# A chunked delta-rule recurrence on one core: two runs of small matrix products per chunk where there were three

## The chip, the cores and the metric

The kernel runs on one core of a Trainium2 chip. Its engines work side by side, each with an instruction queue of its own: PE multiplies matrices (PEld is its weight load), DVE, ACT and POOL do elementwise work, SP issues DMA transfers (ACT and POOL issue some too). An engine takes its instructions in the order in which the program gives them; it stands still when the next one waits for a semaphore. The metric is device time in microseconds.

## The reference, cut to what matters

The program is one layer of a decoder over 1024 positions of width 1024: a projection, three branches (the RWKV-7 recurrence, stick-breaking attention, cross-attention into 256 memory tokens), sigmoid gates with an output projection, and a convolutional feed-forward part. The change lies in the recurrence, for 8 heads of 64:

```python
def step(S, inp):
    r_t, w_t, k_t, v_t, kk_t, a_t = inp
    sa = jnp.einsum('bhij,bhj->bhi', S, -kk_t)
    S = (S * w_t[:, :, None, :]
         + sa[..., None] * (kk_t * a_t)[:, :, None, :]
         + v_t[..., None] * k_t[:, :, None, :])
    y_t = jnp.einsum('bhij,bhj->bhi', S, r_t)
    return S, y_t
...
y = rwkv7_recurrence(rh, dh, kh, vh, kk, ah)
```

Everything is float32, and the output is the layer's (1, 1024, 1024).

## The kernel before, in words

**Chunks.** The recurrence is computed in 16 chunks of 64 positions. What needs no state is prepared for all chunks in earlier stages: matrices of decayed products between positions (tiles `L`, read from DRAM into tags `at` and `it`), the values (`V`) and a triangular inverse (`TT`, in tag `qk`). The 8 heads stand as 4 pairs, one head on partitions 0 to 63 and one on 64 to 127. `stage2` (L599) then walks the chunks. For a chunk it does, on PE unless another engine is named, with one PSUM bank per pair (tag `g`, four banks) that is divided into four blocks of 64 columns, A, Y, W and S:

1. *A*: the state's part `ra` x U (8 products, one per head, from chunk 1 on) and on top the part M x v (8). DVE copies A of each pair into `v1` (L656).
2. *W*: the inverse applied to `v1` (8 products). ACT copies each head's W into the value tile, where it stands below the values (L664, 8 copies).
3. *Y* and *S*: the state's part of Y (8), then for each pair Y (2) and S (2), with both halves of the value tile, so of 128 rows. DVE updates the pair's state in place, U = U x decay + S (L674), and ACT copies Y of both heads into the output tile `y` (L676).

Chunk 0 has no state parts, and chunk 15 no S. A step reads what the step before it gave to another engine, and the next chunk's A reads the updated state.

**Large products between.** The steps are a generator; after each step it yields. `weave` takes one step, and then a number of steps of a second generator, `pump`, which does independent work: projections, gates and output products of the branches, six products of 128 x 128 by 128 x 512 at a time (`mm3`, L107). The ratio, 2.08 steps of six per yield, says how many. Every such instruction goes through `pinned` (L124), which with `strict` on fixes the order of each engine as the one in which the Python code emits it; so the code's order in `stage2` is the order on PE, ACT and DVE. All matrix products are recorded at one line, `mmul` (L139): the small ones write tag `g`, the large ones of this stage tag `mm`. `norm_part` yields pieces of the output's group norm (DVE and ACT), of which `next(norm, None)` takes one.

**Waits.** Tiles are tracked by the framework: an instruction that touches a buffer that another engine has read or written gets a semaphore wait for it.

**Around it.** Before `stage2`, `inverse` (L581) runs on DVE in 62 steps on the tile `inst`, which is loaded from `mad` by four DMAs (L578, one per pair, at the end of the preparation), and whose result goes to DRAM as `td` by sixteen DMAs (L597). They are issued by POOL. SP issues nearly all other loads: the weight tiles `wr` (L79) that feed the large products (split by ACT into `wh`, L83, and by POOL into `wl`, L89), the branch outputs `A` (L1261), the tiles `L` (L617).

Of the kernel before, what the change touches and what calls it, by code (L numbers as in the profile page):

```python
# [22 lines left out]
NC = T // C  # L23
# [27 lines left out]
class Trunk:  # L51
# [365 lines left out]
    def rwkv_prep(self, p, krv, need):  # L417
# [160 lines left out]
        nc.gpsimd.dma_start(self.inst[p * 32 : p * 32 + 32], self.mad[p * 32 : p * 32 + 32])  # L578
        yield

    def inverse(self):  # L581
# [11 lines left out]
        for p in range(4):  # L593
            for h2 in range(2):
                for cc in range(2):
                    i0 = p * 32 + h2 * 16 + cc
                    nc.gpsimd.dma_start(self.td[p // 2, :, h2, :, p % 2, cc * 64 : cc * 64 + 64], X[i0 : i0 + 15 : 2])  # L597
                    for _ in range(3):
                        yield  # L599

    def stage2(self):
        nc = self.nc
        self.y = [self.t4("qk") for _ in range(4)]
        uv = self.t4("ys", n=512).rearrange("p (u c) -> p u c", u=8)
        U, v1s = [uv[:, p] for p in range(4)], [uv[:, 4 + p] for p in range(4)]
# [29 lines left out]
        for c in range(NC):  # L635
            g, cc = c // 2, c % 2
            us = []
            for p in range(4):
                L, (V, TT) = Ls[g, p], VTs[g, p]
                us.append((  # L640
                    U[p], L[:, cc * 128 : (cc + 1) * 128], L[:, 256 + cc * 128 : 256 + (cc + 1) * 128],
                    L[:, 512 + cc * 256 : 512 + (cc + 1) * 256], [v[:, cc * 64 : (cc + 1) * 64] for v in V],
                    TT[:, cc * 64 : (cc + 1) * 64], v1s[p], self.ps("g")))

            def state(o, rs):
                for p, h2 in heads if c else ():
                    Up, ra, _, _, _, _, _, pb = us[p]
                    q = hq[h2]
                    self.mmul(pb[q, o], ra[q, rs], Up[q], start=True, stop=False)

            state(A, Y)
            for p, h2 in heads:
                _, _, _, M, wv, _, v1, pb = us[p]
                self.mmul(pb[hq[h2], A], M[hq[h2], h2 * 128 + 64 : h2 * 128 + 128], wv[h2][hq[h2]], start=(c == 0), stop=True)
                if h2 == 1:
                    self.pinned(nc.vector.tensor_copy(v1, pb[:, A]))  # L656
            yield
            next(norm, None)
            for p, h2 in heads:
                _, _, _, _, wv, tt, v1, pb = us[p]  # L660
# [6 lines left out]
            state(Y, A)  # L667
            for p, (Up, ra, bt, M, wv, tt, v1, pb) in enumerate(us):
                for h2, q in enumerate(hq):
                    self.mmul(pb[q, Y], M[:, h2 * 128 : h2 * 128 + 64], wv[h2], start=(c == 0), stop=True)  # L670
                if c < NC - 1:
                    for h2, q in enumerate(hq):
                        self.mmul(pb[q, S], bt[:, q], wv[h2], start=True, stop=True)
                    self.pinned(nc.vector.scalar_tensor_tensor(Up, Up, self.pc[p][:, c : c + 1], pb[:, S], ALU.mult, ALU.add))  # L674
                for h2, q in enumerate(hq):
                    self.pinned(nc.scalar.activation(self.y[p][cc * 64 : cc * 64 + 64, g * 128 + h2 * 64 : g * 128 + h2 * 64 + 64], pb[q, Y], AF.Copy))  # L676
            if cc and g + 2 < NG:
                for p in range(4):
                    load(g + 2, p)
            yield  # L680
            next(norm, None)
# [5 lines left out]
            if c == 13:  # L687
                self.gs = [self.load_gg(p) for p in range(2)]
        for _ in range(3):
# [1277 lines left out]
    def run(self):  # L1967
# [5 lines left out]
        self.bufs_w = {"w4": 3, "A": 4, "qk": 8, "at": 7, "ys": 1, "it": 1}  # L1973
# [72 lines left out]
        self.weave(st2, pump, 2.08, 0)  # L2046
# [83 lines left out]
```

## Time and profile before

| | us |
|---|---|
| time, median of 3 runs | 1788.42 (1787.28 to 1788.75) |
| the profiled execution: span | 1785.0 |
| PE busy in it | 1775.7 |
| window of the recurrence, 784.7 to 980.0 | 195.3 |
| PE busy in that window | 194.56 |

The span of a profiled execution is from its first to its last instruction on the core. It lies 3.4 us below the runs' median, and a time worked out on the span is compared with the runs by adding that.

How to read the rows that follow in the prediction. A *window* row gives start and end, length, and then for PE, PEld, DVE, ACT and POOL the busy time (with the count of instructions), then PE's granted clock, the DMA engines' busy share and GB/s. A row of the *timeline* or of the *chain of waits* gives a start, a duration, the engine (ACTq or SPq is that engine's queue of DMA issues), the line, the operation, output<-input, how many instructions it lumps, and in brackets the idle time before them with what ended it. One small float32 product leaves two records, so `x16` is 8 small products; some records can be missing. Rows of groups give the busy time and the mean of one instruction in ns, then the idle time ahead. `issue` is time in which an engine waited for nothing that the profile shows. A row "PE g L139 <- DVE ys L656" in the view of waits gives the idle time of the first engine that the second ended: the sum, the count and the longest.

### The profile page before, as it was taken

To read this page: it belongs to the slowest core of one execution; us is meant where nothing else is said; L and a number is where in the kernel's file an instruction comes from. 1 tells how busy PE (TensorE), PEld (TensorE's weight loads), DVE (VectorE), ACT (ScalarE), POOL (GpSimd) and SP (SyncE) were. 2 spreads that over 40 slices of the span, in tenths; PEclk is the share of its full clock that TensorE was granted. 3 is DMA by queue.
4 is the path that set the end of the run, shared out by engine and by line. 5 is a ranking of instruction groups with operands and counts; after the bars stand their busy time and mean duration, and the time that the engine had idled before them with its cause. 6 is when DMAs were issued, how large, how long until landed. Compare 5 with 4: busy or idle time off the path is not lost.

```text
span 1785.0 us, 27451 instructions
## 1 busy us (share of the span) xinstructions
PE 1775.7 (99%) x10481; PEld 1442.9 (81%) x10481; DVE 1184.1 (66%) x1687; ACT 882.8 (49%) x1667; POOL 697.1 (39%) x409
## 2 busy tenths in 40 slices
PE   9999999999999999999999999999999999999999
PEld 7777778878888888787777888888888888888887
DVE  5666674787888655243533882697767777795596
ACT  6543344466566635444556434454444445444343
POOL 1232252322221012022333322257777677545454
PEclk9999999999999999999999999999999999999999
DMA  4256574111112343658764662323323333396475
GB/s 185 72 167 188 180 247 152 51 56 43 54 57 69 111 126 93 201 181 280 264 229 146 236 210 98 115 89 124 101 89 110 109 109 113 109 330 219 142 248 200
DMA packets 120758, 263.39 MB, mean 148 GB/s; under 512 B 28330, under 2 KB 41130, under 8 KB 120499
## 3 DMA queue, kind: packets, MB, share of 16 engines
q1 hardware_dynamic: 82434, 193.31, 32.9%
q10 hardware_dynamic: 34416, 55.72, 8.5%
q0 software_dynamic: 3776, 12.62, 2.4%
q8 instruction: 82, 1.34, 0.3%
q14 instruction: 50, 0.40, 0.1%
HBM read 180.04 MB, written 81.53 MB: 147 GB/s over the span
## 4 chain that ended last, share of the span: by engine, by line
PE 62%; issue 1%; POOL 1%; ACT 1%; DVE 1%; DMA 0%; ACTq 0%; DVEq 0%; POOLq 0%; SPq 0%
PE mm L139 53%; PE g L139 8%; PE g L122 1%; POOL dw L1856 1%; DVE qk L715 0%; ACT wh L83 0%; DMA qk<-vd 0%; ACT w L885 0%; DVE w L886 0%; DVE keep L1876 0%; POOL l L1555 0%; ACT qk L664 0%; ACT ys L1020 0%; DVE wl L86 0%; ACT qk L1059 0%
## 5 line engine op out<-in xcount | busy, mean ns | idle before, releaser
L89 POOL TENSOR_TENSOR wl<-wr,wh 128x1024 fp32r<-128x1024 f32 x58 | 148.0, 2552 | 368.2 <-ACT wh L83 360.5
L139 PE MATMUL mm<-xhi,wh 128*128 128x512 f32 x784 | 260.6, 413 | 0.5 <-ACT w L936 0.4
L139 PE MATMUL mm<-xlo,wh 128*128 128x512 f32 x784 | 243.5, 392 | 0.7 <-DVE xlo L225 0.6
L139 PE MATMUL mm<-xhi,wl 128*128 128x512 f32 x784 | 242.2, 390 | 0.0
L139 PEld LDWEIGHTS mm<-xlo,wh 128*128 128x128 f32 x784 | 147.0, 188 | 34.0 <-DVE xlo L225 1.6
L139 PEld LDWEIGHTS mm<-xhi,wl 128*128 128x128 f32 x784 | 147.1, 188 | 32.6
L139 PEld LDWEIGHTS mm<-xhi,wh 128*128 128x128 f32 x784 | 136.5, 189 | 30.4 <-issue 7.9
L139 PE MATMUL mm<-dw,da 128*128 128x512 f32 x528 | 121.1, 390 | 0.0
L83 ACT ACTIVATE wh<-wr 128x1024 fp32r<-128x1024 f32 x75 | 79.5, 1060 | 81.0 <-PE mm L139 61.9
L139 PE MATMUL mm<-BT,l 128*128 128x512 f32 x504 | 118.0, 389 | 0.3 <-POOL l L1555 0.3
L139 PEld LDWEIGHTS mm<-dw,da 128*128 128x128 f32 x528 | 98.9, 188 | 21.7 <-DVE da L1855 1.2
L1856 POOL TENSOR_TENSOR dw<-draw,dw 128x512 fp32r<-128x512 f32 x55 | 83.1, 1520 | 77.0 <-ACT dw L1854 74.2
L985 DVE TENSOR_TENSOR_SCAN at<-at,at 128x128 f32<-128x128 f32 (+3 forms) x64 | 91.0, 1429 | 33.1 <-ACT at L979 33.0
L139 PEld LDWEIGHTS mm<-BT,l 128*128 128x128 f32 x504 | 94.5, 188 | 20.3 <-POOL l L1555 0.7
L139 PE MATMUL mm<-BT,wh 128*128 128x512 f32 x352 | 108.5, 389 | 0.1
L139 PE MATMUL mm<-B,wh 128*128 128x512 f32 x352 | 108.4, 389 | 0.0
L195 POOL TENSOR_TENSOR hf<-rs,half 128x16 f32<-128x16 f32 (+1 forms) x18 | 49.2, 2732 | 143.4 <-DVE rs L192 138.9
L1855 DVE TENSOR_TENSOR da<-draw,da 128x512 fp32r<-128x512 f32 x77 | 66.6, 873 | 49.0 <-ACT da L1853 48.6
L139 PE MATMUL g<-dw,da 128*128 128x512 f32 x396 | 90.5, 389 | 0.4 <-POOL dw L1856 0.4
L1853 ACT ACTIVATE da<-draw 128x512 fp32r<-128x512 f32 x77 | 48.3, 628 | 81.0 <-PE mm L139 31.7
L139 PEld LDWEIGHTS g<-dw,da 128*128 128x128 f32 x396 | 74.2, 188 | 16.2 <-POOL dw L1856 0.8
L1627 ACT ACTIVATE g<-u,params 128x512 f32<-128x512 f32 x88 | 65.2, 770 | 32.1 <-DVE u L1717 22.9
(345 smaller groups left out, 3956.6 us busy)
## 6 DMA issues: line engine op xcount, KB each, us to landing
wr<-in_w_in_dram SPq DMA_DIRECT2D x49, 512.0 KB, 3.8
draw<-actd SPq DMA_DIRECT2D x77, 256.0 KB, 3.1
at<-scr SPq DMA_DIRECT2D x28, 512.0 KB, 5.5
draw<-in_w_down_dram SPq DMA_DIRECT2D x55, 256.0 KB, 4.6
rw<-in_w_up_dram SPq DMA_DIRECT2D x22, 512.0 KB, 3.5
actd<-gall ACTq DMA_DIRECT2D x41, 256.0 KB, 3.1
gsd<-w ACTq DMA_DIRECT2D x20, 512.0 KB, 2.8
wr<-in_w_up_dram SPq DMA_DIRECT2D x18, 512.0 KB, 3.6
```

Source lines behind the costliest of these rows:

```text
L83: ins = self.nc.scalar.activation(hi, raw, AF.Copy)
L89: self.last_wl = self.nc.gpsimd.tensor_tensor(lo, raw, hi.bitcast(F32), ALU.subtract)
L122: self.pinned(self.nc.tensor.transpose(out, in_, self.ident[:n, :n]))
L139: self.pinned(self.nc.tensor.matmul(*a, **k))
L195: nc.gpsimd.tensor_tensor(out, t[:, :n], self.half[:, :n], ALU.pow)
L985: self.pinned(nc.vector.tensor_tensor_scan(sn[:, :W][:, ::-1], sn[:, :W][:, ::-1], self.smask[:, 1024 - W :][:, ::-1], 1.0, ALU.mult, ALU. ...
L1627: keep(nc.scalar.activation(c, u[:, 2 + h * 512 : 514 + h * 512], AF.Identity, scale=self.par("cw2", m), bias=self.par("cb", m)))
L1853: self.pinned(nc.scalar.activation(A[:, 0], a, AF.Copy))
L1855: self.pinned(nc.vector.tensor_tensor(A[:, 1], a, A[:, 0].bitcast(F32), ALU.subtract))
L1856: nc.gpsimd.tensor_tensor(Wt[:, 1], w, Wt[:, 0].bitcast(F32), ALU.subtract)
```

## The change

`stage2` does a chunk's steps in another order and in two runs in place of three. The step A for the next chunk (`head`) is no longer a run of its own: it follows directly on S, Y and the state's part of Y. Within the joined run S of all pairs comes first, then Y of all pairs, then the state's part of Y, pair by pair with ACT's copies, then the next chunk's A, its value part first and the state's part on top. The state has two copies, `uv` and `un`, which take turns (tag `ys` gets two buffers): the update reads one and writes the other, since the state's part of Y is now computed after the update. The four banks are taken once (`banks`), and chunks take turns in their two halves of 256 columns. There are two yields per chunk and one ahead, with 2.95 steps of large products each. The twenty transfers of `inverse` and of its input are issued by SP, and the descriptor area of the DMAs that POOL issues gets another size.

```diff
@@ end of the preparation (L578) and inverse (L597) @@
-        nc.gpsimd.dma_start(self.inst[p * 32 : p * 32 + 32], self.mad[p * 32 : p * 32 + 32])
+        nc.sync.dma_start(self.inst[p * 32 : p * 32 + 32], self.mad[p * 32 : p * 32 + 32])
...
-                    nc.gpsimd.dma_start(self.td[p // 2, :, h2, :, p % 2, cc * 64 : cc * 64 + 64], X[i0 : i0 + 15 : 2])
+                    nc.sync.dma_start(self.td[p // 2, :, h2, :, p % 2, cc * 64 : cc * 64 + 64], X[i0 : i0 + 15 : 2])
@@ stage2 @@
-        uv = self.t4("ys", n=512).rearrange("p (u c) -> p u c", u=8)
-        U, v1s = [uv[:, p] for p in range(4)], [uv[:, 4 + p] for p in range(4)]
+        uv, un = (self.t4("ys", n=512).rearrange("p (u c) -> p u c", u=8) for _ in range(2))
+        U, v1s = [[x[:, p] for p in range(4)] for x in (uv, un)], [uv[:, 4 + p] for p in range(4)]
...
-        for c in range(NC):
+        banks = [self.ps("g") for _ in range(4)]
+
+        def chunk(c):
...
-                    U[p], L[:, cc * 128 : (cc + 1) * 128], L[:, 256 + cc * 128 : 256 + (cc + 1) * 128],
+                    U[c % 2][p], U[1 - c % 2][p], L[:, cc * 128 : (cc + 1) * 128], L[:, 256 + cc * 128 : 256 + (cc + 1) * 128],
...
-                    TT[:, cc * 64 : (cc + 1) * 64], v1s[p], self.ps("g")))
-
-            def state(o, rs):
-                for p, h2 in heads if c else ():
-                    Up, ra, _, _, _, _, _, pb = us[p]
-                    q = hq[h2]
-                    self.mmul(pb[q, o], ra[q, rs], Up[q], start=True, stop=False)
-
-            state(A, Y)
+                    TT[:, cc * 64 : (cc + 1) * 64], v1s[p], banks[p][:, cc * 256 : cc * 256 + 256]))
+            return us
+
+        def head(c, us):
             for p, h2 in heads:
-                _, _, _, M, wv, _, v1, pb = us[p]
-                self.mmul(pb[hq[h2], A], M[hq[h2], h2 * 128 + 64 : h2 * 128 + 128], wv[h2][hq[h2]], start=(c == 0), stop=True)
+                _, _, _, _, M, wv, _, _, pb = us[p]
+                self.mmul(pb[hq[h2], A], M[hq[h2], h2 * 128 + 64 : h2 * 128 + 128], wv[h2][hq[h2]], start=True, stop=(c == 0))
+            for p, h2 in heads:
+                Up, _, ra, _, _, _, _, v1, pb = us[p]
+                if c:
+                    self.mmul(pb[hq[h2], A], ra[hq[h2], Y], Up[hq[h2]], start=False, stop=True)
                 if h2 == 1:
                     self.pinned(nc.vector.tensor_copy(v1, pb[:, A]))
-            yield
-            next(norm, None)
+
+        us = chunk(0)
+        head(0, us)
+        yield
+        for c in range(NC):
+            g, cc = c // 2, c % 2
             for p, h2 in heads:
...
             yield
             next(norm, None)
-            state(Y, A)
-            for p, (Up, ra, bt, M, wv, tt, v1, pb) in enumerate(us):
-                for h2, q in enumerate(hq):
-                    self.mmul(pb[q, Y], M[:, h2 * 128 : h2 * 128 + 64], wv[h2], start=(c == 0), stop=True)
-                if c < NC - 1:
+            if c < NC - 1:
+                for p, (Up, Un, _, bt, _, wv, _, _, pb) in enumerate(us):
                     for h2, q in enumerate(hq):
                         self.mmul(pb[q, S], bt[:, q], wv[h2], start=True, stop=True)
-                    self.pinned(nc.vector.scalar_tensor_tensor(Up, Up, self.pc[p][:, c : c + 1], pb[:, S], ALU.mult, ALU.add))
+                    self.pinned(nc.vector.scalar_tensor_tensor(Un, Up, self.pc[p][:, c : c + 1], pb[:, S], ALU.mult, ALU.add))
+            for p, (_, _, _, _, M, wv, _, _, pb) in enumerate(us):
                 for h2, q in enumerate(hq):
+                    self.mmul(pb[q, Y], M[:, h2 * 128 : h2 * 128 + 64], wv[h2], start=True, stop=(c == 0))
+            for p, (Up, _, ra, _, _, _, _, _, pb) in enumerate(us):
+                for h2, q in enumerate(hq):
+                    if c:
+                        self.mmul(pb[q, Y], ra[q, A], Up[q], start=False, stop=True)
                     self.pinned(nc.scalar.activation(self.y[p][cc * 64 : cc * 64 + 64, g * 128 + h2 * 64 : g * 128 + h2 * 64 + 64], pb[q, Y], AF.Copy))
+            if c < NC - 1:
+                us = chunk(c + 1)
+                head(c + 1, us)
...
-            yield
-            next(norm, None)
+            for _ in range(2):
+                next(norm, None)
...
+            yield
@@ run, main @@
-        self.bufs_w = {"w4": 3, "A": 4, "qk": 8, "at": 7, "ys": 1, "it": 1}
+        self.bufs_w = {"w4": 3, "A": 4, "qk": 8, "at": 7, "ys": 2, "it": 1}
...
-        self.weave(st2, pump, 2.08, 0)
+        self.weave(st2, pump, 2.95, 0)
...
-    nc = bacc.Bacc("TRN2", target_bir_lowering=False, num_devices=1)
+    nc = bacc.Bacc("TRN2", target_bir_lowering=False, num_devices=1, dynamic_dma_scratch_size=4096)
```

**The order on PE, before.** This is the end of one chunk's third run. `g_7263` to `g_7266` are the banks of the four pairs, `ys` is the state, `at` and `it` are the pair's tile `L`, `qk` its value tile; `Activation_49` and `DVE_49` are the semaphores of ACT and DVE.

```order
L139 MATMUL g_7265<-ys_6790,at_6986 64x64 [waits Activation_49]
L139 MATMUL g_7265<-ys_6790,at_6986 64x64
L139 MATMUL g_7266<-ys_6790,it_6992 64x64 [waits Activation_49]
L139 MATMUL g_7266<-ys_6790,it_6992 64x64
L139 MATMUL g_7263<-qk_6980,at_6978 64x64 x4
L139 MATMUL g_7264<-qk_6980,at_6984 64x64 x4
L139 MATMUL g_7265<-qk_6988,at_6986 64x64 x4
L139 MATMUL g_7266<-qk_6988,it_6992 64x64 x4
L139 MATMUL mm_7381<-yhi_6773,wh_7179 128x512 [waits DVE_49]
```

The state's part of Y stands first; its wait is for ACT's copies of the run before (W), ahead of which twelve large products stand. The sixteen products of Y and S (four per pair) have no wait in front of them, and large products follow.

**The same place on PE after the change.** The run begins with S of the four pairs; the rows are its next part, from the last pair's Y (read off `qk`) to the end of the state's part of Y.

```order
L139 MATMUL g_7029<-qk_6989,it_6993 64x64 [waits DVE_49]
L139 MATMUL g_7029<-qk_6989,it_6993 64x64
L139 MATMUL g_7026<-ys_6790,at_6979 64x64
L139 MATMUL g_7026<-ys_6790,at_6979 64x64 [waits Activation_49]
L139 MATMUL g_7027<-ys_6790,at_6985 64x64
L139 MATMUL g_7027<-ys_6790,at_6985 64x64 [waits Activation_49]
L139 MATMUL g_7028<-ys_6790,at_6987 64x64
L139 MATMUL g_7028<-ys_6790,at_6987 64x64 [waits Activation_49]
L139 MATMUL g_7029<-ys_6790,it_6993 64x64
L139 MATMUL g_7029<-ys_6790,it_6993 64x64 [waits Activation_49]
```

Each pair's Y has a wait for DVE in front of it, which resolves to that pair's state update from the same bank. The second head's state product of each pair waits for ACT, which resolves to the copy of the first head's Y. Right behind these rows, in the same run, stands the next chunk's A, value part:

```order
L139 MATMUL g_7026<-qk_6981,at_6979 64x64 x2
L139 MATMUL g_7027<-qk_6981,at_6985 64x64 x2
L139 MATMUL g_7028<-qk_6989,at_6987 64x64 x2
L139 MATMUL g_7029<-qk_6989,it_6993 64x64 [waits Activation_49]
L139 MATMUL g_7029<-qk_6989,it_6993 64x64
```

Its last pair waits for ACT, which resolves to the copy of that pair's last Y. Eight state products of A follow, and only then large products. The order holds 48 runs of small products before and 33 after, with 744 small products in both, and 18 large ones between most runs where there were mostly 12.

**The order on SP ahead of the recurrence.** Before:

```order
L621 DMA qk_6988<-vd 64x256
L622 DMA qk_6952<-td 128x256
L622 DMA qk_6980<-td 128x256
L1261 DMA A_6730<-yd 128x1024
L1261 DMA A_6732<-yd 128x1024
L79 DMA wr_6826<-in_w_in_dram 128x1024
L617 DMA at_6792<-scr 128x1024
L617 DMA at_6794<-scr 128x1024
L617 DMA at_6796<-scr 128x1024
L617 DMA at_6798<-scr 128x1024
L79 DMA wr_6888<-in_w_br_dram 128x1024
L1261 DMA A_6734<-yd 128x1024
```

And after:

```order
L79 DMA wr_6609<-in_w_in_dram 128x1024
L597 DMA td<-inst 8x64x64 x3
L1273 DMA A_6728<-yd 128x1024
L1273 DMA A_6730<-yd 128x1024
L1273 DMA A_6732<-yd 128x1024
L1273 DMA A_6734<-yd 128x1024
L79 DMA wr_6736<-in_w_in_dram 128x1024
L617 DMA at_6793<-scr 128x1024
```

The sixteen stores `td` have come into this queue, and the weight load `wr_6736`, which before was the row right ahead of those shown and had one of the four loads `A` ahead of it, now stands behind all four.

More of the change, by code (lines that the diff above doesn't have):

```diff
@@ L640, in stage2 @@
                 us.append((
-                    U[p], L[:, cc * 128 : (cc + 1) * 128], L[:, 256 + cc * 128 : 256 + (cc + 1) * 128],
+                    U[c % 2][p], U[1 - c % 2][p], L[:, cc * 128 : (cc + 1) * 128], L[:, 256 + cc * 128 : 256 + (cc + 1) * 128],
                     L[:, 512 + cc * 256 : 512 + (cc + 1) * 256], [v[:, cc * 64 : (cc + 1) * 64] for v in V],
-                    TT[:, cc * 64 : (cc + 1) * 64], v1s[p], self.ps("g")))
-            def state(o, rs):
-                for p, h2 in heads if c else ():
-                    Up, ra, _, _, _, _, _, pb = us[p]
-                    q = hq[h2]
-                    self.mmul(pb[q, o], ra[q, rs], Up[q], start=True, stop=False)
-            state(A, Y)
-            for p, h2 in heads:
-                _, _, _, M, wv, _, v1, pb = us[p]
-                self.mmul(pb[hq[h2], A], M[hq[h2], h2 * 128 + 64 : h2 * 128 + 128], wv[h2][hq[h2]], start=(c == 0), stop=True)
+                    TT[:, cc * 64 : (cc + 1) * 64], v1s[p], banks[p][:, cc * 256 : cc * 256 + 256]))
+            return us
+        def head(c, us):
+            for p, h2 in heads:
+                _, _, _, _, M, wv, _, _, pb = us[p]
[4 more added lines that the diff above has]
+                    self.mmul(pb[hq[h2], A], ra[hq[h2], Y], Up[hq[h2]], start=False, stop=True)
                 if h2 == 1:
                     self.pinned(nc.vector.tensor_copy(v1, pb[:, A]))
-            yield
-            next(norm, None)
+        us = chunk(0)
[3 more added lines that the diff above has]
+            g, cc = c // 2, c % 2
             for p, h2 in heads:
-                _, _, _, _, wv, tt, v1, pb = us[p]
+                _, _, _, _, _, wv, tt, v1, pb = us[p]
                 self.mmul(pb[hq[1 - h2], W], tt[hq[h2]], v1[hq[h2]], start=True, stop=True)
```

## The prediction, made before the changed kernel was run

> **What bounds the kernel now.** I read the page's first part, then the window of the stage that the change touches, then the chain of waits inside it, then who waited for whom on PE.
>
> ```profile
> span 1785.0 us, 27451 instructions
> PE 1775.7 (99%) x10481; PEld 1442.9 (81%) x10481; DVE 1184.1 (66%) x1687; ACT 882.8 (49%) x1667; POOL 697.1 (39%) x409
> 784.70:980.00 195.30, 194.56 (x2051) 152.69 (x2052) 77.24 (x235) 104.16 (x389) 61.78 (x37) 1.00 0.67 230
> 870.31 1.08 PE g L139 x32
> 871.39 2.95 PE mm L139 x12
> 874.34 0.61 PE g L139 x16
> 874.95 4.31 PE mm L139 x18
> 879.26 1.69 PE g L139 x48
> PE g L139 <- DVE ys L656: 0.5, 1, 0.5
> ```
>
> PE is busy 99% of the span, and 194.56 of the 195.30 us of the recurrence (third line: window, then PE, PEld, DVE, ACT and POOL busy). So the time is what PE has to issue plus every wait put in front of it. The next five lines are one chunk: three runs of small products (x16 records are 8 products, two records each) with 12 or 18 large ones between them. Those large products are the cover for the hand-offs between PE, DVE and ACT, and it suffices: in the whole recurrence PE itself waits once for another engine, 0.5 us. Whatever the change does is therefore decided by two questions: what a run costs beyond its products, and whether the hand-offs still lie under large products.
>
> **Part 1, fewer runs: a gain.** 8 products take 0.61 and 16 take 1.08, so 8 more cost 0.47 and a run of small products costs 0.14 more than its products. 18 large products take 4.31 and 12 take 2.95: 0.227 each, so a run of 12 (2.72) costs 0.23 more. A run removed is worth 0.14 + 0.23 = 0.37 us. The issue orders hold 48 runs of small products before and 33 after, with the same 744 products: 15 x 0.37 = **-5.5 us**. The cover ahead of the second and the third step grows from 12 to 18 large products, so what stalls there are go: the window leaves PE 195.30 - 194.56 = 0.74 us idle, **-0.7**.
>
> **Part 2, the hand-offs that now stand inside a run: a loss.** The rows of the issue order quoted with the change show it. In the joined run PE issues S for the four pairs, then Y, then the state part of Y, then the next chunk's A. Four Y products now wait for DVE (its update reads S from the same bank), the second half of each pair's state part waits for ACT (its copy of the first half), and the last pair's A waits for ACT's last copy. Before, PE wrote a pair's Y, state part and S in one go and DVE and ACT read the bank afterwards. What one hand-off takes:
>
> ```profile
> 788.36 0.68 PE L139 MATMUL g<-ys,qk 64*64 64x64 f32 x16
> 788.73 1.88 ACT L664 ACTIVATE qk<-g 64x64 f32<-64x64 f32 x8 [2.47 <-PE g L139]
> 791.91 1.15 PE L139 MATMUL g<-qk,at 128*64 128x64 f32 x32
> 792.49 0.97 DVE L674 SCALAR_TENSOR_TENSOR ys<-ys,pc,g 128x64 f32<-128x64 f32 x4 [5.48 <-PE g L139]
> L676 ACT ACTIVATE qk<-g x128: 216/219/222, 792.8 to 982.9; 64x64 f32<-64x64 f32 x128
> L674 DVE SCALAR_TENSOR_TENSOR ys<-ys,pc,g x60: 269/280/282, 792.5 to 969.7; 128x64 f32<-128x64 f32 x60
> 865.64 0.23 ACT qk L664
> 865.87 0.04 issue
> 865.91 1.41 PE g L139 x36
> 963.48 0.72 PE L139 MATMUL g<-ys,qk 64*64 64x64 f32 x16 [0.46 <-DVE ys L656]
> 964.13 0.73 PE L139 MATMUL mm<-xhi,wh 128*128 128x512 f32 x2
> ```
>
> A small product of 64 rows takes 0.47 / 8 = 0.059; of 128 rows (1.69 - 0.61) / 16 = 0.068. PE to ACT: ACT's copy waits for the second product, which goes off 0.06 after 788.36, and starts at 788.73: 0.31 from that product's start. PE to DVE: the update needs the fourth product after 791.91 (792.11) and starts at 792.49: 0.38. A copy is 0.22 and the next follows at 1.88 / 8 = 0.235; an update is 0.28, the next follows at (0.97 - 0.28) / 3 = 0.23. Back to PE: ACT ends at 865.87, PE starts at 865.91: 0.05.
>
> Y, counted from the first S: the pair's two S products end their issue so that DVE starts at 0.07 + 0.38 = 0.45; the four updates end at 0.73, 0.96, 1.19 and 1.42; the last pair's Y starts at 1.47 and is issued by 1.61. Without waits the 16 products are through at 16 x 0.068 = 1.08. **0.53 per chunk.**
>
> State part and next A: the first pair's second half may start 0.31 + 0.22 + 0.05 = 0.58 after the first. It and the next pair's first half then go off together, ACT makes two copies in a row, and the next second half starts 0.31 + 0.235 + 0.22 + 0.05 = 0.815 later; three times, 2.45. The last copy comes back after another 0.58, and only then may the last pair's A start: 0.58 + 2.45 + 0.58 = 3.61 from the first state product. Without waits 14 products stand there, 14 x 0.059 = 0.83. **2.78 per chunk.**
>
> Chunks 1 to 14 have both: 14 x 3.31 = 46.3. Chunk 0 has no state part, but its Y waits (0.53) and A must wait for eight copies that begin with the first Y (0.78 + 0.07 + 0.31 = 1.16; 1.16 + 1.88 + 0.05 = 3.09 against 1.08 + 6 x 0.059 = 1.43): 1.66. The last chunk has neither S nor A: 0.58 + 2.45 + 0.06 - 0.47 = 2.62. Together **+50.6**. These waits have no cover at all: the large products are queued behind them on PE, and PE passes nothing forward (at 963.48 it stood 0.46 us for DVE with large products next in its order).
>
> After a wait the products restart a little late: at 963.48 a run of 8 gave way to large products after 0.65 against 0.61 without a wait, 0.04. With nine waits in a joined run, 14 x 9 x 0.04 = **+5**.
>
> Copies and updates can also find their engine busy. In the window ACT works 104.16 us, of which 54.3 are these copies (28.0 and 26.3 by the groups below), so other work holds it 50 us, about a fifth of a stage that becomes 245 us long; its usual piece is 1.05.
>
> ```profile
> L664 ACT ACTIVATE qk<-g 64x64 f32<-64x64 f32 x128 | 28.0, 219 | 28.8 <-PE g L139 26.4 <-ACT w L889 0.4
> L676 ACT ACTIVATE qk<-g 64x64 f32<-64x64 f32 x120 | 26.3, 219 | 28.0 <-DVE ys L674 26.0
> L83 ACT ACTIVATE wh<-wr 128x1024 fp32r<-128x1024 f32 x12 | 12.6, 1054 | 14.2 <-issue 13.1 <-POOL hf L195 1.0
> L886 DVE TENSOR_TENSOR w<-w,rbc 128x1024 f32<-128x1024 f32 x5 | 12.5, 2507 | 7.4 <-ACT w L885 7.4
> ```
>
> A fifth of 16 chunks times half a piece is 1.7, and about as much for DVE: **+3**. The bounds are 0 and a whole piece each time, 16 x 1.05 + 5 x 2.5 = 29.
>
> **Part 3, transfers moved from POOL to SP.** Four loads of the inverse's input and its sixteen stores leave POOL (16 x 0.83 us of POOL's time, which is 39% busy) and stand in SP's queue, where a waiting one holds the weight loads behind it.
>
> ```profile
> td<-inst POOLq DMA_DIRECT2D x16, 128.0 KB, 5.2
> mad<-at SPq DMA_DIRECT2D x32, 64.0 KB, 4.5
> wr<-in_w_in_dram SPq DMA_DIRECT2D x49, 512.0 KB, 3.8
> SPq L79 <- POOL wl L89: 444.0, 45, 22.2
> 749.49 0.32 SPq L1261 DMA_DIRECT2D A<-yd  x1
> 743.25 41.61 PE mm L139 x176
> 784.87 0.61 PE g L139 x16
> ```
>
> The four loads each wait for a store to land, 4.5 us. A weight load goes out as soon as a buffer frees, after a mean wait of 444 / 45 = 9.9, two tiles (2 x 48 x 0.227 = 22 us) ahead; 4.5 + 3.8 + the split (1.05 on ACT, 2.55 on POOL by the first group of the page) = 12. Hidden: 0, and 18 if not. Just before the recurrence one weight load now stands behind the load that went out at 749.49. It lands about 754 and is split by 756.5; its first product stands 126 large ones ahead of the recurrence, 28.6 us, which now begins six products later, about 786: 757.6. Hidden by one us; taken as 0, with 2 as the upper bound. Everything else (the second state copy, the halves of a bank, a smaller descriptor area for POOL's 20 fewer transfers) adds no instruction on PE.
>
> **Sum.** +50.6 + 5 + 3 - 5.5 - 0.7 = +52.4 on an execution whose span is 1785.0: 1837.4, and with the 3.4 us by which the runs' median (1788.42) exceeds the span, **1841 us**.
>
> **Rivals.** (a) *The clock drops.* In a joined run PE works about 2.5 us of 5.8.
>
> ```profile
> 1.46 5.66 PE L139 MATMUL g<-qk 128*128 128x512 f32 x13 [1.46 <-DVE qk L202]
> 10.32 0.73 PE L139 MATMUL mm<-xlo,wh 128*128 128x512 f32 x2 [0.59 <-DVE xlo L225]
> 10.89 0.62 PE L139 MATMUL mm<-xhi,wl 128*128 128x512 f32 x2
> ```
>
> The program's first 13 large products took 0.435 each, half speed, after PE had stood idle. If each joined run did that to the 18 large products after it, 14 x 18 x (0.435 - 0.227) = +52: 1893. Against it: after the 0.59 us wait at 10.32 the products went on at full pace, and no single wait here is longer than 0.6. The Trainium skill (TensorE: Matmul & The Clock Gate, What's actually happening) says that a window of 3.4 us without activity halves the clock; the first row agrees with the half, and no run here shows how little activity counts as none.
>
> (b) *Only part of the waits costs.* If the second half's state product did not have to wait for the copy of the first half, since they lie on different partitions, Y's 0.53 would stay, and A's last pair would wait for eight copies after the first state product (0.31 + 1.88 + 0.05 = 2.24 against 0.83): 15 x 0.53 + 14 x 1.41 + 1.1 = 28.8, with the gains 1811. For it: different partitions hold different data. Against: the wait stands in the order that PE gets. The Trainium skill (PSUM — Partial Sum Buffer, PSUM bank collisions raise a hardware error) says that engines may use different 32-partition quadrants of one bank at once, so by that page these four waits a run are not needed; the program has them, and the trace has none of them to show.
>
> (c) *Faster.* The place is the joined run's four state pairs: if ACT's copies came back within the 0.06 us that one product takes, all waits would be covered and the gains alone would stand: 1782. It decides at a hand-off of 0.06, and the shortest here is 0.31 + 0.22 + 0.05.
>
> (d) *SP's queue* holds weight loads late as well: up to 18 + 2, 1861.
>
> **Chances.** Forecast 0.78, (a) 0.08, (b) 0.05, (c) 0.03, (d) 0.04, no change 0.02. About 0.2% is what a measurement of this kernel can tell from no change: faster 0.03, same 0.02, slower 0.95. The range: without restarts, busy engines and Y's waits (15 x 0.53 = 8) the sum is 1841 - 16 = 1825; with both engines busy each time (29 for 3) 1867. I take 1823 to 1868, which leaves out (a), (b) and (c), 0.16.
>
> **What would show it.** In the changed kernel the window of the recurrence is some 45 us longer with the same products; PE waits for ACT L684's copies about 60 times and for DVE's update 60 times where there was one wait; a joined run takes 5.8 us where its parts took 1.69 + 1.08; 15 runs fewer. Large products after a joined run at 0.227 speak against (a). A joined run of 2.7 us would make the forecast wrong, and a new wait ahead of the recurrence for a weight tile would be (d).

## The result and the profile after

| | before | changed |
|---|---|---|
| time, median of 4 runs, us | 1787.85 (1786.89 to 1788.75) | 1864.87 (1864.25 to 1865.96) |
| ratio | | 1.0435, 95% interval 1.0422 to 1.0449 |
| span of the profiled execution | 1785.0 | 1862.2 |

The change costs 77 us, 4.4%. The first part of the changed kernel's page, and the granted clock in its 40 slices (tenths of full speed):

```profile
span 1862.2 us, 27466 instructions
PE 1819.1 (98%) x10481; PEld 1474.8 (79%) x10481; DVE 1181.2 (63%) x1687; ACT 882.1 (47%) x1667; POOL 678.5 (36%) x389
...
PEclk9999999999999999998888899999999999999999
```

PE is busy 43 us longer with the same 10481 instructions, and in five slices, those of the recurrence, its clock is not full. Who waited for whom on PE:

```profile
PE g L139 <- ACT qk L684: 30.0, 60, 1.1
PE mm L139 <- ACT wh L83: 1.9, 1, 1.9
...
PE g L139 <- DVE ys L676: 0.6, 2, 0.4
```

The 60 waits for ACT's copies of Y are there, 30.0 us. The waits for DVE are not in this list, though they cost time too, as the next rows show: the timeline of one joined run of the changed kernel and of what follows.

```profile
810.76 0.61 PE L139 MATMUL mm<-yhi,wl 128*128 128x512 f32 x2
811.30 1.68 PE L139 MATMUL g<-qk,at 128*64 128x64 f32 x32
812.92 0.33 PE L139 MATMUL g<-ys,at 64*64 64x64 f32 x2
813.55 0.33 PE L139 MATMUL g<-ys,at 64*64 64x64 f32 x4 [0.30 <-ACT qk L684]
814.42 0.33 PE L139 MATMUL g<-ys,at 64*64 64x64 f32 x4 [0.54 <-ACT qk L684]
815.29 0.33 PE L139 MATMUL g<-ys,at 64*64 64x64 f32 x4 [0.54 <-ACT qk L684]
816.17 0.28 PE L139 MATMUL g<-ys,at 64*64 64x64 f32 x1 [0.54 <-ACT qk L684]
...
816.35 0.85 PE L139 MATMUL g<-qk,at 64*64 64x64 f32 x11
816.92 0.49 PE L139 MATMUL g<-qk,it 64*64 64x64 f32 x4
817.13 0.92 PE L139 MATMUL g<-ys,at 64*64 64x64 f32 x12
817.77 0.49 PE L139 MATMUL g<-ys,it 64*64 64x64 f32 x4
818.20 1.22 PE L139 MATMUL mm<-yhi,wh 128*128 128x512 f32 x2
819.21 0.86 PE L139 MATMUL mm<-A,wh 128*128 128x512 f32 x2
819.91 0.62 PE L139 MATMUL mm<-yhi,wl 128*128 128x512 f32 x2
```

S and Y, 16 products, take 1.68 where 16 such products took 1.15 in a row before: the 0.53 that Y loses to DVE stands inside this row as busy time. Then come the four waits for ACT. After them something else is seen: the 16 products of the next chunk's A go from 816.27 to 818.20, 0.12 each where they took 0.059, and the first large products are 0.5 apart where they were 0.227. The same stretch in windows of 3.41 us (start and end, length, PE busy, granted clock, DMA share, GB/s):

```profile
784.70:1060.00 275.30, 243.19 (x2087) 0.89 0.52 173
809.48:812.89 3.41, 3.32 (x41) 1.00 0.36 136
812.89:816.30 3.41, 1.48 (x21) 1.00 0.59 86
816.30:819.71 3.41, 3.41 (x38) 0.50 0.98 377
819.71:823.12 3.41, 3.41 (x16) 1.00 0.83 242
```

PE works little in one window, and in the next it has exactly half the clock. Over the stretch of the recurrence the mean is 0.89, so (1 - 0.89) x 275.3 / 0.5 = 61 us of it ran at half clock: 18 windows, a little over one per chunk.

Where the 77 us lie, read off PE's timeline by the first and last product of each run of small products:

| us | before | changed | difference |
|---|---|---|---|
| start of the recurrence | 784.8 | 788.4 | +3.6 (1.4 of it six large products more) |
| runs of small products, summed | 53.7 | 113.0 | +59.3 |
| large products between them (576 and 564) | 142.1 | 152.0 | +9.9 |
| from its end to the span's end | 804.5 | 808.8 | +4.3 (1.4 of it six large products more) |

564 large products at full clock take 135.2 (the second and third experiment with the same order show 135.3 and 135.2), so the half clock costs 152.0 - 135.2 = 16.8 in them. In the small products it costs less than A's pace above suggests: in five of the joined runs of chunks 1 to 14, A is through, or all but through, before the half clock begins. One of the five in the timeline, and then the window behind it:

```profile
1014.90 1.63 PE L139 MATMUL g<-qk,at 128*64 128x64 f32 x32
...
1019.70 0.27 PE L139 MATMUL g<-ys,at 64*64 64x64 f32 x1 [0.54 <-ACT qk L684]
...
1020.85 0.28 PE L139 MATMUL g<-ys,it 64*64 64x64 f32 x4
1021.07 1.22 PE L139 MATMUL mm<-xhi,wh 128*128 128x512 f32 x2
...
1021.07:1024.49 3.42, 3.42 (x12) 0.50 0.88 327
```

These five runs take 6.17 to 6.30 us, the nine others, with A at half clock, 6.76 to 7.90. With 6.24 as the length at full clock, the 14 runs are 7.0 us longer than 14 x 6.24; 1.2 of that are late engines in two runs, and the last chunk's run adds some 0.3: about 6 us for the half clock in the small products, and 16.8 + 6 = 23 in all. What is left of the small products' 59.3 is the hand-offs: 59.3 - 6 + 15 x 0.14 (the runs saved) = 55 us. So the 77 us are 55 for the hand-offs and 23 for the clock, less 6 for the fewer runs, and 5 ahead of and behind the recurrence (3.6 + 4.3, less 2.7 for the twelve large products that stand there now). Ahead of it the cause is the late weight tile of experiment 6; behind it 2.9 us are left, and their cause stays open.

### The profile page after: what moved, and what is told of

It is laid out like the page before. It is cut to its first block, busy times and chain, and to the rows that moved or that the text cites. A ratio compares the mean times of both kernels' runs of the same rounds, so it can differ in the third digit from the quotient of the medians.

```text
span 1862.2 us, 27466 instructions
## 1 busy us (share of the span) xinstructions
PE 1819.1 (98%) x10481; PEld 1474.8 (79%) x10481; DVE 1181.2 (63%) x1687; ACT 882.1 (47%) x1667; POOL 678.5 (36%) x389
## 4 chain that ended last, share of the span: by engine, by line
PE 52%; issue 2%; ACT 1%; POOL 1%; DVE 0%; DVEq 0%; POOLq 0%; ACTq 0%
PE mm L139 44%; PE g L139 8%; POOL dw L1868 1%; ACT qk L684 1%; PE g L122 1%; DVE ys L676 0%; ACT qk L669 0%; DVE keep L1888 0%; POOL l L1567 0%; ACT w L897 0%; ACT l L1566 0%; DVE w L1309 0%; DVE gall L1647 0%; ACT sg L1644 0%; DVEq L2129 0%
## 5 line engine op out<-in xcount | busy, mean ns | idle before, releaser
L139 PE MATMUL mm<-xhi,wh 128*128 128x512 f32 x784 | 265.6, 420 | 2.3 <-ACT wh L83 1.9
L139 PE MATMUL mm<-xlo,wh 128*128 128x512 f32 x784 | 247.4, 397 | 0.2
```

Of the source, the lines that this page charges most:

```text
L139: self.pinned(self.nc.tensor.matmul(*a, **k))
```

## The experiments

The first theory at this point was that three things make up the loss: the waits inside the joined run, the half clock that follows from too little work on PE, and the transfers on SP. The rivals: 40 small products in a row lower the clock whatever they wait for; the half clock costs nothing because PE waits anyway; the joining itself is the loss.

**1. All state products of Y first, then the copies.**

```diff
                 for h2, q in enumerate(hq):
                     if c:
                         self.mmul(pb[q, Y], ra[q, A], Up[q], start=False, stop=True)
+            for p, (_, _, _, _, _, _, _, _, pb) in enumerate(us):
+                for h2, q in enumerate(hq):
                     self.pinned(nc.scalar.activation(self.y[p]..., pb[q, Y], AF.Copy))
```

> All eight state products of Y are issued first, and ACT's eight copies come after them in the code; the rest is the changed kernel. First theory: the waits of the second half's state product go (60 waits, 30 us in the changed kernel); what is left is Y behind DVE (0.53 a chunk) and the last pair's A behind eight copies (0.31 + 1.88 + 0.05 = 2.24 against 0.83, 1.41 a chunk): 15 x 0.53 + 14 x 1.41 + 1.1 = 28.8, less the gains of 6.2, plus the 2.1 of the late weight load: 1788 + 25 = 1813 us; PE is then used more than half in every stretch of 3.4 us, so the granted clock stays at 1.00. Rival, the clock drops because of 40 small products in a row and not because of waits: the same with 30 us more, 1843, clock about 0.89 in the recurrence. Rival, these waits are covered anyway: 1865.

Measured: 1817.64 us, ratio 1.0175 (1.0157 to 1.0194). The same run in its timeline:

```profile
812.38 1.68 PE L139 MATMUL g<-qk,at 128*64 128x64 f32 x32
813.99 0.68 PE L139 MATMUL g<-ys,at 64*64 64x64 f32 x16
814.88 1.27 PE L139 MATMUL g<-qk,at 64*64 64x64 f32 x12 [0.21 <-ACT qk L686]
816.29 0.33 PE L139 MATMUL g<-qk,it 64*64 64x64 f32 x4
816.46 0.52 PE L139 MATMUL g<-ys,at 64*64 64x64 f32 x12
```

The state products are through in half a microsecond, A waits for the eight copies, and A then goes at full clock. Moving one line of the loop gives back some 46 of the 77 us, though 1.4 us of waits per run remain; in the recurrence the clock stays full but for one window. The small products sum to 82.1, 30.5 above the 51.6 of a kernel without waits (53.7 less 15 x 0.14); 28.8 was worked out.

**2. The copies behind the next chunk's A.**

```diff
+            done = us
             if c < NC - 1:
                 us = chunk(c + 1)
                 head(c + 1, us)
+            for p, (_, _, _, _, _, _, _, _, pb) in enumerate(done):
+                for h2, q in enumerate(hq):
+                    self.pinned(nc.scalar.activation(self.y[p]..., pb[q, Y], AF.Copy))
```

(The copies are gone from where they stood.)

> As the run before, but ACT's eight copies of Y stand behind the next chunk's A in the code, so that no product of the joined run has to wait for ACT. First theory: only Y behind DVE is left, 15 x 0.53 = 8: 1788 - 6.2 + 2.1 + 8 = 1792 us, clock 1.00, joined run about 3.3 us. Rival, 40 small products in a row lower the clock: 1822, clock about 0.89.

Measured: 1800.46 us, ratio 1.0079 (1.0061 to 1.0097). Joined runs take 3.16 us, as a run of 2.63 without waits (experiment 4) and 0.53 for Y make it. Of the 8 us that the expectation missed, 5.7 are one place:

```profile
PE g L139 <- DVE ys L676: 6.3, 4, 4.4
```

In the joined run of chunk 5 the state update is 4.4 us late, because DVE has other work of its own order ahead of it (8.82 us in place of 3.16, with a window of half clock in it). Before, twelve large products stood between the update and the product that needs it.

**3. The waits filled with work.** Between the two state products of a pair PE gets extra small products, whose results nobody reads.

```diff
                         self.mmul(pb[q, Y], ra[q, A], Up[q], start=False, stop=True)
+                        if h2 == 0:
+                            for _ in range(8 if p else 7):
+                                self.mmul(us[(p + 2) % 4][-1][hq[0], W], us[p][4][:, 0:64], us[p][5][0], ...)
```

> The changed kernel with 7 or 8 more small products (128 rows, 0.068 us each, on data that is there, into a block of PSUM that is free and read by nobody) between the two state products of each pair, where PE waits for ACT. They fill the wait (0.5 to 0.7 us) and lengthen nothing by themselves. First theory, the clock drops where PE is used too little in a stretch of 3.4 us: the waits for ACT stay, the granted clock is 1.00, and the time falls by the clock's part, about 25 to 30 us: 1835 to 1840 us. Rival, the clock drops with the waits themselves or with small products: clock 0.89 as before, 1865 us or more. Rival, the clock costs nothing because PE waits anyway: clock 1.00 and 1865 us.

Measured: 1870.31 us, ratio 1.0470 (1.0451 to 1.0489). By the time alone the third rival would stand. The trace says why it does not follow:

```profile
813.06 0.33 PE L139 MATMUL g<-ys,at 64*64 64x64 f32 x2
813.31 1.03 PE L139 MATMUL g<-qk,at 128*64 128x64 f32 x14
814.27 0.33 PE L139 MATMUL g<-ys,at 64*64 64x64 f32 x4
814.53 1.15 PE L139 MATMUL g<-qk,at 128*64 128x64 f32 x16
```

Seven extra products, all to the same 64 columns, took 0.96, 0.14 each; the fill ran past the wait's end, and a joined run became 8.2 us. The clock was full all through, and the large products were back at 135.2. So the clock's part was won and lost again to a fill that was too long: this run does not decide between the theories, and experiment 5 has a shorter fill.

**4. One bank per block.**

```diff
-                    TT[:, cc * 64 : (cc + 1) * 64], v1s[p], banks[p][:, cc * 256 : cc * 256 + 256]))
+                    TT[:, cc * 64 : (cc + 1) * 64], v1s[p], [x[:, cc * 256 + p * 64 : cc * 256 + p * 64 + 64] for x in banks]))
...
-                self.mmul(pb[hq[h2], A], M[...], wv[h2][hq[h2]], start=True, stop=(c == 0))
+                self.mmul(pb[A][hq[h2]], M[...], wv[h2][hq[h2]], start=(p == 0), stop=(c == 0), skip_group_check=True)
...
                     for h2, q in enumerate(hq):
-                        self.mmul(pb[q, S], bt[:, q], wv[h2], start=True, stop=True)
+                        self.mmul(pb[S][q], bt[:, q], wv[h2], start=True, stop=True)
+                for p, (Up, Un, _, _, _, _, _, _, pb) in enumerate(us):
-                    self.pinned(nc.vector.scalar_tensor_tensor(Un, Up, self.pc[p][:, c : c + 1], pb[:, S], ALU.mult, ALU.add))
+                    self.pinned(nc.vector.scalar_tensor_tensor(Un, Up, self.pc[p][:, c : c + 1], pb[S], ALU.mult, ALU.add))
```

A, W and Y are changed in the same way: eight products of all pairs, then the copies. In a bank in which several pairs' sums are open at once, only the first pair's products carry the start flag.

> The joined run with another layout: one PSUM bank holds one block (A, Y, W or S) of all four pairs instead of one pair's four blocks, and the copies and updates of a block stand behind its eight products. So Y does not share a bank with what DVE reads, nor A with what ACT reads, and the run has no wait but that of A's state part for the new state, which DVE ends about 1.9 us after the first S, when that product stands at 2.0 or later. First theory (waits inside the run, and the clock that they lower, are the whole loss): the gains alone and the late weight load, 1788 - 6.2 + 2.1 = 1784 us, faster than the kernel before by 0.2%; joined run 2.7 us, clock 1.00. Rival, joining is bad by itself (40 small products in a row lower the clock): about 1814 us, clock 0.89.

Measured: 1790.03 us, ratio 1.0018 (1.0009 to 1.0027). A joined run of it:

```profile
833.62 0.57 PE L139 MATMUL g<-qk,at 128*64 128x64 f32 x12
...
834.71 0.56 PE L139 MATMUL g<-ys,at 64*64 64x64 f32 x12
...
835.22 0.63 PE L139 MATMUL g<-qk,at 64*64 64x64 f32 x16
835.69 0.63 PE L139 MATMUL g<-ys,at 64*64 64x64 f32 x16
836.25 0.73 PE L139 MATMUL mm<-yhi,wh 128*128 128x512 f32 x2
```

2.63 us from first to last, where the changed kernel takes 6.9, and the clock is full behind it. So 40 small products in a row do not lower the clock, and joining the runs is not what costs: that rival falls. Some 74 of the 77 us are the layout and the order inside the run, with what they do to the clock; experiments 1 and 2 show what the place of the copies gives without the layout. The rest of the distance to 1784 is one run of 5.10 (chunk 5 again, 2.5 us too long), the half-clock window behind it (1.6), and what the moved transfers cost beyond the 2.1 us put in for them (experiments 6 and 9).

**5. The fill again, shorter.**

```diff
+                        if h2 == 0:
+                            for i in range(4 if p else 3):
+                                self.mmul(us[(p + 2) % 4][-1][hq[i % 2], W.start : S.stop], us[p][4][:, 0:64], us[p][4][:, 0:128], ...)
```

> The fill of the waits once more, shorter: in the run before each of the 7 or 8 extra products took 0.13 and not 0.07 us (they all added to the same 64 columns), so that they ran past the wait's end and the joined run took 8.2 us in place of 6.8. Now 3 or 4 products of 128 columns, on two halves of the partitions in turn. By their 0.13 us they end at about the time when ACT's copy is back (0.13 to get going + 4 x 0.13 = 0.65 against 0.58 to 0.7). First theory: clock 1.00, the large products after a joined run are back at 4.31 from 5.1, the next chunk's A at 0.95 from 1.9: 1.7 us a chunk, about 26 us in all: 1838 us, up to 1845 if the fill is 0.1 too long each time. Rival, the half clock lies only where PE waits anyway: clock 1.00 and 1865.

Measured: 1844.95 us, ratio 1.0323 (1.0304 to 1.0342), 20 us less than the changed kernel, with more work on PE and the same waits in the program. Windows of 3.4 us at one joined run, the columns as above:

```profile
811.20:814.60 3.40, 3.31 (x41) 1.00 0.33 120
814.60:818.00 3.40, 3.40 (x48) 1.00 0.61 94
818.00:821.40 3.40, 3.40 (x45) 1.00 1.00 389
```

The window of the waits is now filled, and the one behind it has its full clock. The four state pairs still take 3.46 us (3.25 in the changed kernel), so the fill lengthens a run by about 0.2, 3 us in all. In the trace the recurrence takes 245.3 us where it took 265.0; 19.7 and these 3 make some 23 us for the clock, as much as was read off the changed kernel's trace. That the half clock comes from too little work in the window ahead of it, and that it costs about this much, is shown.

**6. The transfers alone, in the kernel before.**

```diff
-        nc.gpsimd.dma_start(self.inst[p * 32 : p * 32 + 32], ...)
+        nc.sync.dma_start(self.inst[p * 32 : p * 32 + 32], ...)
...
-                    nc.gpsimd.dma_start(self.td[p // 2, :, h2, ...], ...)
+                    nc.sync.dma_start(self.td[p // 2, :, h2, ...], ...)
...
+    nc = bacc.Bacc("TRN2", ..., dynamic_dma_scratch_size=4096)
```

> The kernel before with nothing but the twenty transfers of the inverse and its input on SP in place of POOL, and the smaller descriptor area. First theory: one weight tile comes late ahead of the recurrence, as in the changed kernel where PE waited 1.9 us for ACT's split of it and 0.25 for the other half: 1786.4 + 2.1 = 1788.5 us, wait in the trace at about 758 us. Rival, the queue is hidden in the kernel before (its loads of the branch outputs stand elsewhere among SP's issues): 1786.4. Rival, it also costs what the run with a bank per block lost behind the recurrence (2.4 us): 1791.

Measured: 1791.25 us, ratio 1.0022 (1.0013 to 1.0031): 4 us, twice the expected. The wait is where it was in the changed kernel:

```profile
757.18 0.62 PE L139 MATMUL mm<-xhi,wl 128*128 128x512 f32 x2
759.69 0.74 PE L139 MATMUL mm<-xhi,wh 128*128 128x512 f32 x2 [1.89 <-ACT wh L83]
760.26 0.62 PE L139 MATMUL mm<-xlo,wh 128*128 128x512 f32 x2
761.14 0.73 PE L139 MATMUL mm<-xhi,wl 128*128 128x512 f32 x2 [0.25 <-DVE wl L86]
```

2.1 us of the 4 are seen there as idle time. Compared product by product with the kernel before, PE falls 2.7 us behind at this place, so 0.6 more stand there as slow starts. From there to the end of the recurrence nothing is added; about 0.5 comes behind it. That is all that the profiled execution lost, 3.3 us; it was 1.1 us faster than the median of its runs.

**7. Three runs again, with the order of the joined run.**

```diff
             if c < NC - 1:
+                yield
                 us = chunk(c + 1)
                 head(c + 1, us)
...
-        self.weave(st2, pump, 2.95, 0)
+        self.weave(st2, pump, 2.08, 0)
```

> The changed kernel with a yield between Y's state part and the next chunk's A, so three runs a chunk again (ratio 2.08, 12 large products between); order within the runs, banks and copies as in the changed kernel. First theory (the hand-offs that the order and the shared banks put inside the run are the loss, not the joining): waits of 0.53 for DVE and 2.0 for ACT remain, the last pair's A gets cover: 15 x 0.53 + 14 x (2.62 - 0.4) = 39, no gain from fewer runs, 2 for the queue, and the clock's 20 to 30 as before: 1848 to 1858 us, clock about 0.9 in the recurrence. Rival, the joining is the loss: about 1790 us.

Measured: 1874.54 us, ratio 1.0489 (1.0469 to 1.0508). It is slower than the changed kernel by 10 us: undoing the joining alone makes it worse, so that rival falls here too. The third run takes 5.1 us and more in place of 1.69, with 30.5 us of waits for ACT and, new, 5.1 for DVE, and the large products take 164.7 where they took 142.1, so the half clock costs 23 us in them alone. The upper end of the expectation was 16 us too low: it had no wait for DVE beyond the 0.53 of each run, and too little for the hand-offs to ACT (a third run of 5.1 us, where 1.69 + 0.53 + 2.22 = 4.44 was put in).

**8. The bank-per-block kernel, transfers on POOL, two steps of large products earlier.**

```diff
+        for _ in range(2):
+            next(pump)
         self.weave(st2, pump, 2.95, 0)
```

(and the two edits of the sixth experiment undone, but for the descriptor area.)

> The bank-per-block kernel with the twenty transfers back on POOL, and with two more steps of large products ahead of the recurrence, so that DVE's four splits of a branch output (1.2 us each) no longer stand right ahead of a state update: there that kernel lost 2.5 us in one joined run (5.10 against 2.63) and 1.5 us in the half clock that followed. First theory: 1790.0 - 2.1 (queue) - 4.0 = 1784 us, 0.998 of the kernel before, and all joined runs at 2.6 us, clock 1.00. Rival, the late work shows up in another place: 1787 to 1790 us.

Measured: 1793.14 us, ratio 1.0029 (1.0018 to 1.0041). A miss: the run of chunk 5 fell to 3.44, but three others rose to 4.39, 5.80 and 4.02. One of them:

```profile
929.09 2.33 DVE L900 TENSOR_TENSOR w<-w,rbc 128x1024 f32<-128x1024 f32 x1 [7.32 <-issue]
...
931.35 1.86 DVE L729 TENSOR_SCALAR qk<-qk,hn,hf 128x64 f32<-128x64 f32 x8
...
933.13 0.85 DVE L677 SCALAR_TENSOR_TENSOR ys<-ys,pc,g 128x64 f32<-128x64 f32 x4
933.46 0.91 PE L139 MATMUL g<-ys,at 64*64 64x64 f32 x16 [2.73 <-DVE ys L677]
```

The shift moved other work of DVE ahead of other state updates. In a joined run an update has the 24 products between S and A's state part as cover, 1.5 us; any longer piece of DVE that stands ahead of it shows on PE.

**9. The bank-per-block kernel with only the transfers back on POOL.**

> The bank-per-block kernel (1.0018 of the kernel before) with nothing but its twenty transfers back on POOL. The queue alone cost the kernel before 0.22%, 4 us. First theory: joined runs as in that kernel, 2.63 each and one of about 5.1 behind DVE's splits, no wait for ACT's weight split ahead of the recurrence: 0.9996 of the kernel before, 1786 to 1787 us (its gain of 6.2 from fewer runs less the 4 of that one run, to 2 us faster). Rival, the transfers on POOL put other work late: 1790.

Measured: 1784.21 us, ratio 0.9985 (0.9976 to 0.9995). Faster than the kernel before, and 0.3% below experiment 4, which differs in the queue alone. The recurrence begins at 785.8 in place of 788.6, and its clock is full all through although the run of chunk 5 still takes 5.10. So 1.6 us of the difference are not the transfers' own doing: in experiment 4 the waits of that run fell into one window of 3.41 us, which PE's products filled to 0.25, and half clock followed; in experiment 9 no window is filled below 0.50.

**10. The same with a shift around one place.** Steps are pulled forward at chunks 3 and 4 and given back at 5 and 6; the first line stands at the yield behind W, the second at the one behind the joined run.

```diff
+            self.bump = {4: 1, 6: -1}.get(c, 0)
             yield
...
+            self.bump = {3: 1, 5: -1}.get(c, 0)
             yield
...
-            acc += ratio
+            acc += ratio + getattr(self, "bump", 0)
+            self.bump = 0
```

> The same with two steps of large products brought forward around chunks 3 and 4 and taken back around 5 and 6, so that three of DVE's four splits (1.2 us each) stand before the chunk's W and not right ahead of its state update; elsewhere the order is that of the run beside it. First theory: the joined run of chunk 5 falls from 5.1 to 3 us or less and there is no half clock behind it: 3 to 4 us faster than the run beside it, 1783 us, 0.998 of the kernel before. Rival, another 128x1024 product of DVE (2.3 us) that the shift brings to the same place takes their part: no difference.

Measured: 1783.35 us, ratio 0.9978 (0.9969 to 0.9988), faster than the kernel before by 3.6 us. The run of chunk 5 takes 3.44. Its page:

```profile
span 1779.8 us, 27266 instructions
PE 1770.7 (99%) x10481; PEld 1442.8 (81%) x10481; DVE 1183.4 (66%) x1687; ACT 881.7 (50%) x1667; POOL 698.1 (39%) x409
```

The runs of small products sum to 51.4. Between this and experiment 9 the intervals overlap, so the shift's own worth is not shown by the times.

## Why the prediction was right, and where it fell short

Forecast and measured: 1841 and 1864.9 us; 52 and 77 us slower. The direction and the main mechanism, hand-offs that stand inside the joined run without cover, were right. The 24 us that are missing are the half clock, 23 us, which the forecast took for a rival and left out, and 5 us ahead of and behind the recurrence; the hand-offs themselves were put 4 us too high (58.6 with restarts and busy engines, against 55).

That 1864.9 lies inside the stated range, 1823 to 1868, is luck. The upper part of the range was room for busy engines (29 us for the 3 in the sum), which came to little over 1 us; what filled it was the clock, which the range left out with a chance of 0.08.

- **Fewer runs, -5.5 and -0.7: right.** It is seen by itself only where no hand-off stands in the joined run. In experiment 10 the small products sum to 51.4 (53.7 - 15 x 0.14 = 51.6 was forecast), and the recurrence takes 186.8 us with 12 large products fewer than the 195.7 before: 195.7 - 186.8 - 12 x 0.227 = 6.2.
- **Y behind DVE, 0.53 a chunk: right.** 1.68 against 1.15 for the same 16 products, and 3.16 against 2.63 for a joined run without and with a bank per block (experiments 2 and 4).
- **State part and A behind ACT, 2.78 a chunk: right in kind, and in size as far as it can be read.** The waits shown are 0.30 and three of 0.54; the forecast's steps were 0.58 from a product to the next pair's start and 0.815 between pairs, and the rows of the run start at 812.92, 813.55, 814.42, 815.29 and 816.17, 0.63 and 0.87 apart. The last wait, for the last copy, is not seen as idle time. But a joined run at full clock takes 6.24 against 2.63 without waits (experiment 4), 3.6 more; 0.53 + 2.78 = 3.31 of that was worked out. Experiment 1 took the first kind away and kept the second, and came to 30.5 of waits and restarts where the pieces gave 28.8.
- **Restarts (+5) right in size, busy engines (+3) too high.** The 3.6 of a run exceed the 3.31 by 0.3, where nine restarts of 0.04 had been put at 0.36. Of busy engines little is seen: the run of chunk 5 is 1.1 us longer by its waits for DVE and ACT, that of chunk 7 by 0.2.
- **SP's queue, taken as 0 with 2 as bound: too small.** Alone it costs 4 us. The late weight load was the right place, with 2.1 us; the working had it hidden by one us.
- **The step that failed is the reading of rival (a).** "Against it: after the 0.59 us wait at 10.32 the products went on at full pace, and no single wait here is longer than 0.6." The clock does not go by a single wait. It went by the share of a 3.41 us window in which PE worked, and in a joined run five waits stand one after the other, so that little more than 8 products of 0.059, 0.47 us, were what PE did in such a window. The rival was also priced wrongly, at all 18 products behind each run, 52 us: the half clock lasts one window of 3.41 us (two in three places), so it took a part of A's products and a few large ones, 23 us in all. So the forecast and (a) were not alternatives: the waits and the clock add, 55 and 23.

The Trainium skill (TensorE: Matmul & The Clock Gate, HAM oscillation — how this bites in real kernels) puts the rule as no idle gap of PE above about 3.4 us. Here the longest wait in the recurrence was 1.1 us, so by that sentence the clock would have stayed full; the trace shows half clock in 18 windows, and the measurement decides. The Trainium skill (the same page, A second HAM failure mode: psum-queue depth-cycling) tells of a kernel whose PE pauses briefly but often between groups of products and loses its clock in turns. The trace agrees with that: the waits here are 0.30 to 1.1 us each, and the clock goes down and up 15 times.

Rival (b), that the second half's product need not wait for the copy of the first, falls for this program: the product does wait, 60 times and 30.0 us. Whether the program could do without that wait was not tested. Rival (c), that the gains alone remain, is not what the changed kernel does. A bank per block comes near it: experiment 10 is 3.6 us faster than the kernel before, where the gains were put at 6.2. Rival (d), late weight loads, is there with 4 us of the up to 20 that it was priced at.

## What to carry to other kernels

When runs of small products are joined, list what each product in the joined run shares with another engine, PSUM banks included: in this program a bank that holds what another engine is reading orders PE behind that engine even where the columns differ, and giving each stage a bank (all heads' A, all heads' Y) lets the run go through unbroken. Sum the waits by the window and not one by one: several short hand-offs in a row cost their own time once, and then half the clock in what follows. And work that was safe behind twelve large products needs looking at again once only 24 small ones cover it, down to the other pieces in that engine's queue.

## What the runs showed of the hardware

- Half clock came in stretches of 3.41 us (or twice that), beginning on a grid of 3.41 us. Counting in each window the products issued, at 0.059, 0.068 and 0.227 us each, a window of the changed kernel with a share of 0.15 to 0.43 was followed by half clock (15 times), and one with 0.47 or more by full clock. Counted in the same way, the kernel before stays at 0.67 and above all through the recurrence. The bound is not sharp: in experiment 7 a window of 0.39 kept the clock, and in experiment 8 one of 0.47 lost it.
- At half clock a window of the changed kernel that was 0.64 to 0.66 full was followed by another one at half clock (three times), and one that was full, or nearly, by full clock.
- Extra products of 128 rows that all added to the same 64 columns took 0.14 us each, where Y's and S's products, which go to different places in turn, take 0.068. Whether the shared columns are the cause was not tried.
- A wait of PE can stand in the profile as busy time: Y's four waits for DVE, 0.53 a run, are in no row of the view of waits, and show only as 32 records that take 1.68 in place of 1.15.
